# One weight sum of the seven-product blocks, moved from VectorE to GpSimd

## The chip, the cores and the metric

The kernel runs on one core of a Trainium2 chip. The metric is the device time of one execution in microseconds; of several runs the median is given. Profiles are of one execution each.

## What is computed

One decoder layer on 256 tokens of width 2048, in fp32: a SwiGLU feed-forward (width 5632) added at half weight, a token mixer, a second such feed-forward, and a final RMS norm. What matters here is the feed-forward:

```python
def swiglu_ffn(x, w_gate, w_up, w_down):
    return (jax.nn.silu(x @ w_gate) * (x @ w_up)) @ w_down

x = x + FFN_RESIDUAL_SCALE * swiglu_ffn(rms_norm(x, ffn1_norm[l]),
                                        ffn1_w_gate[l], ffn1_w_up[l], ffn1_w_down[l])
...                                     # the mixer
x = x + FFN_RESIDUAL_SCALE * swiglu_ffn(rms_norm(x, ffn2_norm[l]),
                                        ffn2_w_gate[l], ffn2_w_up[l], ffn2_w_down[l])
```

## The kernel before

**Precision.** Every fp32 matrix product is made of three products of a rounded type (fp32r). A weight tile is loaded raw by SyncE's DMA queue (SP), as 128 partitions by 4 x 512 columns (1 MB). ScalarE casts it to a high part `hi` in two halves of 1024 columns, VectorE subtracts it from the raw tile to get the low part `lo` in one instruction of 2048 columns, and TensorE multiplies hi by hi, hi by lo and lo by hi (`parts_of`, `multiply`). In the profile these are `hi_g_p`, `lo_g_p` and so on: g, u, d for the gate, up and down weights; `_p` for the products of the blocks described next, `_x` for their usual products, and no suffix for tiles outside the blocks.

**Seven products for eight.** For pairs of 512-row by 512-column weight tiles in a 2 x 2 arrangement (rows r0, r1; two column groups), `seven` computes the product of a 2 x 2 block of token tiles with a 2 x 2 block of weight tiles in seven products, at the price of sums of weight tiles. The token side's sums are made once (`seven_of`). The weight side has four sums in each block, in this order:

- `w11 = w12 - w11`, in two halves of 1024 columns, for product 4;
- `w11 = w22 - w11`, for product 5;
- `w12 = w22 - w12`, for product 6;
- `w11 = w21 - w11`, for product 3: this is the fourth.

Each writes over a raw tile, which is then cast and split as above. Between them stand the usual products of two further row tiles (`b2`, `b3` with the second column group, `a2`, `a3` with the first). The order of TensorE's work in a block is product 0, 4, b2, 5, b3, 6, 2, a2, 3, a3, 1. TensorE adds up in four PSUM banks a, c, e, d; ScalarE copies some of them out.

**Where blocks stand.** Each feed-forward runs five steps, each with a gate block and an up block over two column groups of 512; after the first, third and fifth step a down block is run over the hidden units so far. That makes 5 x 2 + 3 = 13 blocks in each feed-forward, 26 in all. The mixer between the two feed-forwards uses no such blocks.

**Tiles.** `w11` and `w12` stand in a pool of two buffers of their own (`kept`), the other raw tiles of a block in a pool of three (`raws`). The next block's `w11` takes the buffer of this block's `w12`, and the next block's `w12` that of this block's `w11`, so its load on SP waits until the lo of product 3 is made. `w21` takes one of the three buffers of `raws` and is read by the fourth sum and then, as it is, by product 1. The hi and lo tiles have three buffers.

**Order.** A planner lays the queue of each engine by its own costs and by what it takes to be ready; the engines then work their queues in order and wait for each other through semaphores. A few instructions are pinned behind what was issued ahead of them on their engine (`keep_in_program_order`). In the gate blocks of the third and fifth step of each feed-forward (`order=True`) the two halves of product 4's lo and the sum `w12 - ...` of product 6 are pinned. The fourth sum isn't.

ScalarE, VectorE and TensorE are called through a thin wrapper (class `Engine`), so their instructions all appear at line 43, and groups are told apart by the names of tiles. `nc.gpsimd` is called directly.

Of the kernel before, what the change touches and what calls it, by code (L numbers as in the profile page):

```python
# [14 lines left out]
ALU = mybir.AluOpType  # L15
# [34 lines left out]
def hybrid_block(ctx: ExitStack, tc: tile.TileContext, a: dict, out: bass.AP):  # L50
    nc = tc.nc
    Engine.pinned = False
    dve, act, pe = (Engine(tc, e) for e in (nc.vector, nc.scalar, nc.tensor))
# [29 lines left out]
    def bank(name):  # L83
        return psum.tile([P, 512], F32, tag="ps", name=name)

    def f32(ap):
        return ap.bitcast(F32)
# [71 lines left out]
    def load(src, name, pieces=((0, UK),), loaded=None, kept=False):  # L159
        if kept:  # L160
            raw = extra[1].tile([P, UK, CW], F32, tag="kept", name=f"raw_{name}", bufs=2)
        else:
            raw = raws.tile([P, UK, CW], F32, tag="raw", name=f"raw_{name}")
        for i, e in pieces:
            nc.sync.dma_start(raw[:, i:e, :], src[i * P : e * P].rearrange("(j p) c -> p j c", p=P))
            if loaded:
                loaded(i)
        return raw

    def splits_of(name):  # L170
        pool, bufs = splits, 2
        if extra:
            turn_of["split"] += 1
            if turn_of["split"] % 3 == 0:
                pool, bufs = extra[0], 1
        hi = pool.tile([P, UK, CW], F32R, tag="hi", name=f"hi_{name}", bufs=bufs)
        lo = pool.tile([P, UK, CW], F32R, tag="lo", name=f"lo_{name}", bufs=bufs)
        return hi, lo, [(hi[:, j, :], lo[:, j, :]) for j in range(UK)]

    def parts_of(raw, name, pieces=((0, 2), (2, UK)), split=None):  # L180
        hi, lo, blk = splits_of(name)
        for i, e in pieces:
            if split:
                split(i)
            act.copy(hi[:, i:e, :], raw[:, i:e, :])
            if split:
                dve.tensor_tensor(lo[:, i:e, :], raw[:, i:e, :], f32(hi[:, i:e, :]), op=ALU.subtract)
        if not split:
            dve.tensor_tensor(lo, raw, f32(hi), op=ALU.subtract)
        return blk  # L190
# [4 lines left out]
    def stationary(tile, t):  # L195

        return [(tile[:, j, t * P : (t + 1) * P], tile[:, j, S + t * P : S + (t + 1) * P]) for j in range(UK)]
# [33 lines left out]
    def multiply(targets, blk, apart=False, middle=None):  # L231


        more = dict(skip_group_check=True) if apart else {}
        for ps, st, begin, _ in targets:
            for j in range(UK):
                pe.matmul(ps, st[j][0], blk[j][0], start=begin and j == 0, stop=False, **more)
                pe.matmul(ps, st[j][1], blk[j][0], start=False, stop=False, **more)
        if middle:
            middle()  # L240
        for ps, st, _, end in targets:
            for j in range(UK):
                pe.matmul(ps, st[j][0], blk[j][1], start=False, stop=end and j == UK - 1, **more)
        if len(targets) == NT:
            onward()
# [159 lines left out]
    def seven(w, rows, cols, sf, xs, name, keep, done, between=None, ready=None, whole=True, order=False):  # L405


        a, c, e, d = (bank(f"ps_{name}_{n}") for n in "aced")

        def get(u, n, kept=False):  # L410
            src = w[u * UK * P : (u + 1) * UK * P, cols[n] : cols[n] + CW]
            return load(src, f"{name}_{u}{n}", kept=kept)

        (r0, r1), two = rows, len(xs) > 1
        w11, first = ready or (get(r0, 0, True), None)
        w12 = get(r0, 1, True)
        b2, w22 = get(xs[0][0], 1), get(r1, 1)
        b3 = get(xs[1][0], 1) if two else None
        a2, w21 = get(xs[0][0], 0), get(r1, 0)
        a3 = get(xs[1][0], 0) if two else None  # L420

        def snap(ps, n):
            s = keep(f"{n}_{name}")
            act.copy(s, ps)
            return s

        def product_of(i, raw, ps, begin=False, end=True, blk=None):
            multiply([(ps, sf[i], begin, end)], blk or parts_of(raw, f"{name}_p{i}"), True)

        def usual(i, raw, n, *targets):  # L430

            blk = parts_of(raw, f"{name}_x{i}{n}")
            multiply([(ps, stationary(xs[i][1], t), b, z) for ps, t, b, z in targets], blk, True)

        product_of(0, w11, a, True, blk=first)
        s1 = None if whole else snap(a, "s1")
        if whole:
            act.copy(d, a)
        hi, lo, blk = splits_of(f"{name}_p4")
        for i in (0, 2):  # L440
            o = slice(i, i + 2)
            dve.tensor_tensor(w11[:, o], w12[:, o], w11[:, o], op=ALU.subtract)
            act.copy(hi[:, o], w11[:, o])
        for i in (0, 2):
            o = slice(i, i + 2)
            ins = dve.tensor_tensor(lo[:, o], w11[:, o], f32(hi[:, o]), op=ALU.subtract)
            if order:
                tc.keep_in_program_order(ins)
        product_of(4, w11, c, True, blk=blk)
        s5 = snap(c, "s5")  # L450
        if between:
            between(0)
        usual(0, b2, 1, (e, 1, True, not two), (c, 0, False, False))
        if between:
            between(1)
        dve.tensor_tensor(w11, w22, w11, op=ALU.subtract)
        product_of(5, w11, a)
        u2 = snap(a, "u2")
        if between:
            between(2)  # L460
        if two:
            usual(1, b3, 1, (e, 1, False, True), (c, 0, False, False))
        ins = dve.tensor_tensor(w12, w22, w12, op=ALU.subtract)
        if order:
            tc.keep_in_program_order(ins)
        product_of(6, w12, a)
        u3 = snap(a, "u3")
        done(1, 1, e, [u3, s5])
        product_of(2, w22, c)
        done(0, 1, c, [u2])  # L470
        usual(0, a2, 0, (d, 0, not whole, False), (a, 1, False, False))
        dve.tensor_tensor(w11, w21, w11, op=ALU.subtract)
        product_of(3, w11, a, end=not two)
        if two:
            usual(1, a3, 0, (a, 1, False, True), (d, 0, False, False))
        done(1, 0, a, [])
        product_of(1, w21, d)
        done(0, 0, d, [] if whole else [s1])

    def ffn(tag, norm, after, opening=False):  # L480
        with (
# [252 lines left out]
            def down(last):  # L734
# [64 lines left out]
                if tag == 1 and m == 5:  # L799
                    prepare()  # L800
                seven(
                    wd, (m, n), (2 * CW, CW), sh, [(u, hidden[u]) for u in others], f"d{tag}_{m}", keep, add,
                    within,
# [6 lines left out]
            for s in range(5):  # L810
                cs = (CW + 2 * s * CW, 2 * CW + 2 * s * CW)
                sg = {}

                def total(ps, tiles):
                    for p in tiles[1:]:
                        dve.tensor_tensor(tiles[0], tiles[0], p, op=ALU.add)
                    if not tiles:
                        return ps
                    dve.tensor_tensor(tiles[0], ps, tiles[0], op=ALU.add)
                    return tiles[0]  # L820

                def gate(t, n, ps, tiles):
                    g = total(ps, tiles)
                    sg[t, n] = tiles[0] if tiles else keep(f"z{tag}_{s}")
                    act.activation(sg[t, n], g, AF.Silu)

                def up(t, n, ps, tiles):
                    dve.tensor_tensor(sg[t, n], total(ps, tiles), sg[t, n], op=ALU.mult)
                    turn_hidden(1 + 2 * s + n, t, sg[t, n], s % 2 == 0)

                def meanwhile(i):
                    if s == 0 and not opening and i != 1:
                        (sums, lambda: normalise(3))[i // 2]()

                seven(wg, (0, 1), cs, sf, xs, f"g{tag}_{s}", keep, gate, meanwhile, ready.pop() if ready else None,
                      s > 0 and (tag, s) != (1, 3), s in (2, 4))
                seven(wu, (0, 1), cs, sf, xs, f"u{tag}_{s}", keep, up)
                if s % 2 == 0:
                    down(s == 4)
# [357 lines left out]
```

## Time and profile before

| | |
|---|---|
| median of 2 runs | 1712.8 us (1712.59 to 1713.0) |
| profiled execution, span | 1710.3 us |
| around the span | 2.5 us to the median |
| TensorE (PE) busy | 1693.6 us, 99% |
| VectorE (DVE) busy | 1480.7 us, 87% |
| ScalarE (ACT) busy | 1174.6 us, 69% |
| GpSimd (POOL) busy | 6.9 us |
| granted TensorE clock | 0.999 |
| DMA | 358.96 MB, 210 GB/s |

Times in the views are microseconds from the span's start. A row of the timeline gives start, duration, engine, line, operation, out<-in, shapes and count; in brackets stands the idle time of the engine just ahead of it and what ended it. A row that ends in x2 or x4 merges that many instructions. A row of the groups gives busy time and the mean of one in ns, then the engine's idle time ahead of the group. A row of the waits gives who waited for whom: total, times, longest.

### The profile page before, as it was taken

How to read it: one execution, taken by the hardware profiler on the slowest of the kernel's cores; microseconds unless marked ns; L12 is line 12 of the kernel's file. 1: busy time of each engine (PE TensorE's matmuls, PEld its weight loads, DVE VectorE, ACT ScalarE, POOL GpSimd, SP SyncE). 2: the span in 40 equal slices, each digit the busy share in tenths (PEclk: the TensorE clock that was granted, in tenths of full speed). 3: DMA queues.
4: the chain of work that ended last, by engine and by line, in shares of the span. 5: the costliest groups of instructions: out<-in, count | busy, mean ns of one | idle time of the engine just before them, and what ended most of it. 6: DMA issues, size and time to landing. Idle time of an engine off the chain costs nothing.

```text
span 1710.3 us, 20215 instructions
## 1 busy us (share of the span) xinstructions
PE 1693.6 (99%) x7795; PEld 1411.2 (83%) x7795; DVE 1480.7 (87%) x1297; ACT 1174.6 (69%) x1493; POOL 6.9 (0%) x32
## 2 busy tenths in 40 slices
PE   8999999999999999999999999999999999999997
PEld 6888888888888888888888888888888888888886
DVE  7998988989889879787986669989989888889796
ACT  7867667776567678775655777686567675677764
POOL 1000000000000000000000000000000000000000
PEclk9999999999999999999999999999999999999999
DMA  8666567585567684855555684685666766566753
GB/s 307 204 230 196 197 222 221 191 281 185 181 210 208 224 267 144 247 172 191 177 191 176 221 273 163 209 275 180 216 219 205 215 197 221 197 215 203 243 200 123
DMA packets 237280, 358.96 MB, mean 210 GB/s; under 512 B 68996, under 2 KB 71424, under 8 KB 237056
## 3 DMA queue, kind: packets, MB, share of 16 engines
q1 hardware_dynamic: 236720, 356.55, 64.6%
q8 instruction: 61, 1.00, 0.2%
q10 hardware_dynamic: 144, 1.05, 0.2%
q14 instruction: 35, 0.29, 0.0%
q0 software_dynamic: 320, 0.07, 0.0%
HBM read 339.82 MB, written 2.10 MB: 200 GB/s over the span
## 4 chain that ended last, share of the span: by engine, by line
PE 92%; ACT 3%; DVE 2%; issue 1%; DMA 1%; SPq 0%; DVEq 0%; ACTq 0%
PE ps_d L43 14%; PE ps_in L43 13%; PE ps_g_a L43 8%; PE ps_u_a L43 8%; PE ps_u_c L43 6%; PE ps_d_a L43 5%; PE ps_o L43 5%; PE ps_g_c L43 5%; PE ps_g_d L43 5%; PE ps_d_c L43 3%; PE ps_u_d L43 3%; PE ps_u_e L43 3%; PE ps_u L43 3%; PE ps_d_d L43 3%; PE ps_g_e L43 2%; PE ps_g L43 2%
## 5 line engine op out<-in xcount | busy, mean ns | idle before, releaser
L43 ACT CAST hi_u_p<-raw_u 128x1024 fp32r<-128x1024 f32 x140 | 141.5, 1047 | 54.4 <-DVE raw_u L43 25.7
L43 ACT CAST hi_g_p<-raw_g 128x1024 fp32r<-128x1024 f32 x132 | 134.0, 1047 | 56.4 <-DVE raw_g L43 27.9
L43 DVE TENSOR_TENSOR lo_u_p<-raw_u,hi_u_p 128x2048 fp32r<-128x2048 f32 (+1 forms) x80 | 160.1, 2020 | 14.1 <-ACT hi_u_p L43 13.6
L43 DVE TENSOR_TENSOR lo_g_p<-raw_g,hi_g_p 128x2048 fp32r<-128x2048 f32 (+1 forms) x75 | 151.7, 2033 | 18.5 <-ACT hi_g_p L43 17.7
L43 PE MATMUL ps_d<-hi_d,h 128*128 128x512 f32 x704 | 167.0, 389 | 0.0
L43 PEld LDWEIGHTS ps_d<-hi_d,h 128*128 128x128 f32 x704 | 132.1, 188 | 27.4
L43 PE MATMUL ps_in<-xT_nm,hi_in 128*128 128x512 f32 x640 | 153.1, 391 | 0.0
L43 PEld LDWEIGHTS ps_in<-xT_nm,hi_in 128*128 128x128 f32 x640 | 117.5, 188 | 23.0 <-ACT tha L43 0.4
L43 DVE TENSOR_TENSOR lo_d<-raw_d,hi_d 128x2048 fp32r<-128x2048 f32 x44 | 100.2, 2289 | 34.9 <-ACT hi_d L43 34.8
L43 ACT CAST hi_d_p<-raw_d 128x1024 fp32r<-128x1024 f32 x84 | 86.2, 1048 | 63.7 <-DVE raw_d L43 23.3
L43 ACT CAST hi_in<-raw_in 128x1024 fp32r<-128x1024 f32 x80 | 80.1, 1046 | 59.3 <-PE ps_in L43 45.8
L43 DVE TENSOR_TENSOR lo_in<-raw_in,hi_in 128x2048 fp32r<-128x2048 f32 x40 | 91.4, 2287 | 33.6 <-ACT hi_in L43 33.3
L43 ACT CAST hi_u_x<-raw_u 128x1024 fp32r<-128x1024 f32 x80 | 81.3, 1047 | 38.9 <-PE ps_u_c L43 26.6
L43 DVE TENSOR_TENSOR lo_d_p<-raw_d,hi_d_p 128x2048 fp32r<-128x2048 f32 (+1 forms) x48 | 96.5, 2021 | 7.6 <-ACT hi_d_p L43 7.3
L43 ACT CAST hi_d<-raw_d 128x1024 fp32r<-128x1024 f32 x88 | 88.9, 1045 | 18.5 <-PE ps_d_d L43 7.6
L43 DVE TENSOR_TENSOR raw_u<-raw_u,raw_u 128x2048 f32<-128x2048 f32 (+1 forms) x50 | 92.3, 1863 | 10.3 <-DMA raw_u<-in_ffn_w_up_dram 9.7
L43 DVE TENSOR_TENSOR lo_g_x<-raw_g,hi_g_x 128x2048 fp32r<-128x2048 f32 x40 | 91.5, 2288 | 10.4 <-ACT hi_g_x L43 10.4
L43 ACT CAST hi_g_x<-raw_g 128x1024 fp32r<-128x1024 f32 x80 | 81.2, 1046 | 24.3 <-DMA raw_g<-in_ffn_w_gate_dram 10.8
L43 DVE TENSOR_TENSOR lo_u_x<-raw_u,hi_u_x 128x2048 fp32r<-128x2048 f32 x40 | 91.4, 2286 | 1.2 <-ACT hi_u_x L43 1.2
L43 DVE TENSOR_TENSOR raw_g<-raw_g,raw_g 128x2048 f32<-128x2048 f32 (+1 forms) x46 | 85.1, 1871 | 5.8 <-DMA raw_g<-in_ffn_w_gate_dram 5.6
L43 PE MATMUL ps_d<-lo_d,h 128*128 128x512 f32 x352 | 87.3, 389 | 0.0
L43 PEld LDWEIGHTS ps_in<-xT_nm,lo_in 128*128 128x128 f32 x640 | 82.1, 191 | 3.1
(408 smaller groups left out, 3678.7 us busy)
## 6 DMA issues: line engine op xcount, KB each, us to landing
raw_d<-in_ffn_w_down_dram SPq DMA_DIRECT2D x88, 1024.0 KB, 5.7
raw_u<-in_ffn_w_up_dram SPq DMA_DIRECT2D x87, 1024.0 KB, 5.3
raw_g<-in_ffn_w_gate_dram SPq DMA_DIRECT2D x86, 1024.0 KB, 5.4
raw_in<-in_w_in_dram SPq DMA_DIRECT2D x40, 1024.0 KB, 5.1
raw_o<-in_w_out_dram SPq DMA_DIRECT2D x16, 1024.0 KB, 5.1
xres<-in_x_dram SPq DMA_DIRECT2D x4, 512.0 KB, 7.6
raw_u<-in_ffn_w_up_dram SPq DMA_DIRECT2D x2, 512.0 KB, 9.4
raw_g_first<-in_ffn_w_gate_dram SPq DMA_DIRECT2D x1, 1024.0 KB, 11.9
```

What stands on the lines that cost most here:

```text
L43: ins = getattr(self.engine, name)(*args, **kwargs)
```

## The change

The fourth weight sum of every block is issued to GpSimd's queue in place of VectorE's. Operands, tile and operation are the same.

```diff
         product_of(2, w22, c)
         done(0, 1, c, [u2])
         usual(0, a2, 0, (d, 0, not whole, False), (a, 1, False, False))
-        dve.tensor_tensor(w11, w21, w11, op=ALU.subtract)
+        nc.gpsimd.tensor_tensor(w11, w21, w11, op=ALU.subtract)
         product_of(3, w11, a, end=not two)
         if two:
             usual(1, a3, 0, (a, 1, False, True), (d, 0, False, False))
```

## The prediction

> **What bounds the kernel now.** I read the page from the top: busy times and the chain that ended last; then PE's waits, because an engine that is 99% busy can only lose or gain what it idles.
>
> ```profile
> span 1710.3 us, 20215 instructions
> ...
> PE 1693.6 (99%) x7795; PEld 1411.2 (83%) x7795; DVE 1480.7 (87%) x1297; ACT 1174.6 (69%) x1493; POOL 6.9 (0%) x32
> ...
> PE 92%; ACT 3%; DVE 2%; issue 1%; DMA 1%; SPq 0%; DVEq 0%; ACTq 0%
> ```
>
> TensorE is the bound: 1693.6 of 1710.3 us, and 92% of the chain. It idles 16.7 us in all, most of it at the two ends of the kernel. VectorE is the fullest of the others, but 229.6 us of its span are free, and ScalarE has more. GpSimd (POOL) has next to nothing to do. So the question is not how much work moves, but whether a piece that TensorE needs comes later than it is needed.
>
> ```profile
> PE ps_g_a L43 <- DVE lo_g_p L43: 1.8, 4, 0.6
> ```
>
> This row of PE's waits is the only one in which TensorE waits for VectorE: 1.8 us, in four waits of 0.6 us at most. That is the whole visible prize for unloading VectorE.
>
> **The change part by part. What goes.** One subtract per block leaves VectorE's queue. The two groups below (by shape) hold the whole-tile weight sums of the up and gate products.
>
> ```profile
> L43 DVE TENSOR_TENSOR raw_u<-raw_u,raw_u 128x2048 f32<-128x2048 f32 x30 | 68.7, 2290 | 8.9 <-DMA raw_u<-in_ffn_w_up_dram 8.5
> L43 DVE TENSOR_TENSOR raw_g<-raw_g,raw_g 128x2048 f32<-128x2048 f32 x28 | 63.9, 2288 | 5.8 <-DMA raw_g<-in_ffn_w_gate_dram 5.6
> ```
>
> Up has ten blocks with three whole-tile sums each, which is the x30; gate has ten as well (the first tile of two of them has another name), and down has six: 26 blocks. So VectorE is freed of 26 x 2.29 = 59.5 us and falls to about 1421 us, 83%. It also no longer stands in line for the fourth sum's operand: most of the 8.5 and 5.6 us of idle time above are VectorE at the head of its queue waiting for w21 to land. None of this is on the path, since TensorE does not wait for it; its value is at most the 1.8 us above.
>
> **What comes.** 26 GpSimd instructions of 128x2048 fp32, two inputs. The trace has no such instruction; the nearest rows are these.
>
> ```profile
> L1005 POOL MEMSET zx<- 128x3 f32 x8 | 0.6, 100 | 729.5 <-ACT pair L43 690.8 <-DVE xc L43 38.4 <-ACT xs L43 0.3
> ...
> masks.py:199 POOL TENSOR_SCALAR_AFFINE_SELECT ident<-ident 128x128 f32<-128x128 f32 x1 | 0.3, 313 | 0.1
> masks.py:197 POOL MEMSET ident<- 128x128 f32 x1 | 0.2, 204 | 0.3 <-POOLq L1184 0.3
> ```
>
> A memset costs 100 ns for nothing and (204 - 100) / 125 = 0.83 ns per column written. One read and one write cost (313 - 100) / 128 = 1.66 ns per column, so a read adds 0.83. For 2048 columns: 3.5 us if the second read runs beside the first, 100 + 2048 x 2.49 = 5.2 us if it is a third pass. Neither end is nearer, so I estimate R = 4.4 us, the middle, against VectorE's 2.29. [...]
>
> **Where the latency falls.** GpSimd's queue holds nothing else here (its memsets belong to the mixer), so the instruction starts when w21 lands. Behind it wait, on ScalarE, the two hi casts of product 3 and the casts and PSUM copies queued after them; then VectorE's lo of product 3; then TensorE; and on SP the next block's w12, whose tile that lo frees. A typical gate block, VectorE and then TensorE:
>
> ```profile
> 464.33 2.29 DVE L43 TENSOR_TENSOR raw_g<-raw_g,raw_g 128x2048 f32<-128x2048 f32 x1 [1.60 <-DMA raw_g<-in_ffn_w_gate_dram]
> 466.54 2.28 DVE L43 TENSOR_TENSOR lo_g_p<-raw_g,hi_g_p 128x2048 fp32r<-128x2048 f32 x1
> ...
> 473.14 2.28 DVE L43 TENSOR_TENSOR lo_g_p<-raw_g,hi_g_p 128x2048 fp32r<-128x2048 f32 x1
> ```
>
> ```profile
> 472.71 1.07 PE L43 MATMUL ps_g_c<-lo_g_p,xs 128*128 128x512 f32 x4
> ...
> 480.87 1.07 PE L43 MATMUL ps_g_a<-lo_g_p,x 128*128 128x512 f32 x4
> ```
>
> The fourth sum runs at 464.33, as w21 lands. The lo at 466.54 belongs to product 2, read at 472.71; the one at 473.14 to product 3, done at 475.42 and read at 480.87: 5.45 us early. A sum that ends R - 2.29 = 2.1 us later is covered by that. In one place it is not:
>
> ```profile
> 1085.43 2.29 DVE L43 TENSOR_TENSOR raw_g<-raw_g,raw_g 128x2048 f32<-128x2048 f32 x1
> ...
> 1088.17 3.88 ACT L43 CAST hi_g_p<-raw_g 128x1024 fp32r<-128x1024 f32 x4
> ...
> 1090.19 4.49 DVE L43 TENSOR_TENSOR lo_g_p<-raw_g,hi_g_p 128x2048 fp32r<-128x2048 f32 x2 [0.27 <-ACT hi_g_p L43]
> ...
> 1092.55 1.17 PE L43 MATMUL ps_g_a<-lo_g_p,x 128*128 128x512 f32 x4
> ```
>
> This is the first gate block of the second FFN. The sum ends at 1087.72, two casts run from 1088.17 to 1090.1, the first lo ends at about 1092.45, TensorE reads it at 1092.55: nothing to spare but the 0.45 us ahead of the casts and the 0.2 us by which GpSimd may start sooner. Cost: about R - 2.8 = 1.6 us.
>
> **What the two engines do to each other.** No row shows GpSimd reading a large tile while VectorE works, so this is an unknown with two ends. One end: they do not disturb each other, and the bill is the 1.6 us. The other end: they take turns, and VectorE stands still for R. Then the next VectorE instruction, which starts 2.2 us after the fourth sum's start today, is late by R - 2.2 = 2.2 us, and what counts is how early it is needed. In the block above product 2's lo ends 3.9 us before its use (468.82 to 472.71): nothing lost. Eight blocks have this order; the first and the last of them, VectorE's row and TensorE's:
>
> ```profile
> 114.18 2.29 DVE L43 TENSOR_TENSOR lo_u_p<-raw_u,hi_u_p 128x2048 fp32r<-128x2048 f32 x1
> ```
>
> ```profile
> 120.57 1.07 PE L43 MATMUL ps_u_c<-lo_u_p,xs 128*128 128x512 f32 x4
> ```
>
> ```profile
> 1510.72 2.28 DVE L43 TENSOR_TENSOR lo_u_p<-raw_u,hi_u_p 128x2048 fp32r<-128x2048 f32 x1
> ```
>
> ```profile
> 1517.28 1.07 PE L43 MATMUL ps_u_c<-lo_u_p,xs 128*128 128x512 f32 x4
> ```
>
> They are 4.1 and 4.3 us early. The tight ones are the gate blocks whose order is pinned, four of them, the first and the last shown:
>
> ```profile
> 298.56 2.29 DVE L43 TENSOR_TENSOR raw_g<-raw_g,raw_g 128x2048 f32<-128x2048 f32 x1 [0.53 <-DMA raw_g<-in_ffn_w_gate_dram]
> 300.77 4.49 DVE L43 TENSOR_TENSOR lo_g_p<-raw_g,hi_g_p 128x2048 fp32r<-128x2048 f32 x2
> ```
>
> ```profile
> 303.57 1.07 PE L43 MATMUL ps_g_a<-lo_g_p,xs 128*128 128x512 f32 x4
> ```
>
> ```profile
> 1552.89 4.49 DVE L43 TENSOR_TENSOR lo_g_p<-raw_g,hi_g_p 128x2048 fp32r<-128x2048 f32 x2
> ```
>
> ```profile
> 1556.30 1.07 PE L43 MATMUL ps_g_a<-lo_g_p,xs 128*128 128x512 f32 x4
> ```
>
> Here product 6's lo comes next, is done at 303.05 and 1555.15 (half of each pair), and is read 0.5 and 1.1 us later; with about 0.9 as the mean, each of the four costs R - 3.1 = 1.3 us, 5.2 together. Turns therefore cost 1.6 + 5.2 = 6.8 us at R = 4.4, 2.3 at 3.5 and 10.8 at 5.2. Below nothing, the 1.8 us are the limit. Between the ends 1.6 and 6.8 no row decides; I take 4, the middle.
>
> [...]
>
> **The sum**: 1710.3 + 4 = 1714.3 for the span. The medians' 1712.8 lies 2.5 us above the profiled span (what is around it), so 1717 on the clock that counts.
>
> **The rivals.**
> *Hidden altogether*: no turns, the tight place absorbed or the 1.8 us won. For it: the 229.6 us of free VectorE time and 5.45 us of lead. Against it: the 0.1 us of lead at 1092.55. 1711 to 1714.
> *The queues come out in another order*: the planner lays each queue by its own costs, and a piece that sits on another engine shifts what is ready when. For it: TensorE idles so little that the present order is a good one, and pieces with leads of 0.1 and 0.5 us exist. Against it: the data dependences are the same. If in 8 of 26 blocks a tight lo comes behind one more 2.29 us instruction, 8 x 2.2 = 18 us: 1731; I give it 1722 to 1746.
> *A slow GpSimd with turns, slower by over 2%*: with the two engines taking turns, every block begins to pay beyond a certain R: the eight blocks like 464.33 from R = 2.2 + 3.9 = 6.1 us, and four up blocks, the first and the last below, from 2.2 + 3.6 = 5.8 (the next piece ends at 347.97 and 1601.02, read at 351.62 and 1604.57):
>
> ```profile
> 345.69 2.28 DVE L43 TENSOR_TENSOR lo_u_x<-raw_u,hi_u_x 128x2048 fp32r<-128x2048 f32 x1
> ```
>
> ```profile
> 351.62 1.07 PE L43 MATMUL ps_u_d<-lo_u_x,x 128*128 128x512 f32 x4
> ```
>
> ```profile
> 1598.74 2.28 DVE L43 TENSOR_TENSOR lo_u_x<-raw_u,hi_u_x 128x2048 fp32r<-128x2048 f32 x1
> ```
>
> ```profile
> 1604.57 1.07 PE L43 MATMUL ps_u_d<-lo_u_x,x 128*128 128x512 f32 x4
> ```
>
> At R = 7.2: 4 x 4.1 + 4.4 + 8 x 1.1 + 4 x 1.4 = 35 us, 2% of 1712.8 and about what a measurement of this kernel can tell from no change. At R = 9 it is 4 x 5.9 + 6.2 + 8 x 2.9 + 4 x 3.2 = 66 us, 1779. For it: R is not measured. Against it: my rows reach to 5.2.
>
> **How the numbers follow.** Forecast 0.47 (1714 to 1722), hidden 0.22, other order 0.20, slow GpSimd 0.10, faster by over 2% 0.01: that would need 1678.5 us, below the 1693.6 that TensorE is busy. Slower by over 2% is 0.10, within 2% the remaining 0.89. The range 1710 to 1740 (its low end is the hidden case's 1711 less the 0.4 us between the runs, rounded down) leaves out the slow GpSimd, the top of the other order (0.05) and the 0.01.
>
> **What would show it.** Right: 26 POOL subtracts of 3.5 to 5.2 us at line 472; VectorE near 1421 us busy, or longer by stretched instructions if there are turns; PE still near 1693.6 busy; its waits for VectorE up from 1.8 to about 6, in the pinned gate blocks and near 1092. Turns would show as lo instructions beside a POOL subtract that take 4 us or more instead of 2.29, or start only at its end. Wrong: POOL subtracts of 7 us; TensorE waiting for hi casts in ordinary blocks; a new order of TensorE's products.

## The result, and the profile after

The median of two runs is 1757.94 us (1756.49 to 1759.39) against 1712.8, a ratio of 1.0263 with a 95% interval of 1.0234 to 1.0293. The kernel is 2.6% slower, and the time lies 18 us above the range that was given.

The page of the changed kernel, span and busy times:

```profile
span 1757.6 us, 20241 instructions
...
PE 1708.4 (97%) x7795; PEld 1412.7 (80%) x7795; DVE 1491.4 (85%) x1271; ACT 1172.5 (67%) x1493; POOL 153.2 (9%) x58
```

The number to stop at is VectorE's. It has 26 instructions fewer (1297 to 1271), worth 59.5 us, and is busy for 10.7 us **more**. So some 70 us of its busy time are instructions that stand still: they wait after they have started, and the profile counts that as busy (the lo at 265.94 below stands with 6.49 us in place of 2.29). GpSimd's groups by shape:

```profile
L472 POOL TENSOR_TENSOR raw_u<-raw_u,raw_u 128x2048 f32<-128x2048 f32 x10 | 56.4, 5639 | 370.6 <-DMA raw_u<-in_ffn_w_up_dram 370.6
L472 POOL TENSOR_TENSOR raw_g<-raw_g,raw_g 128x2048 f32<-128x2048 f32 x9 | 52.2, 5804 | 575.9 <-DVE raw_g L43 321.7 <-DMA raw_g<-in_ffn_w_gate_dram 254.3
L472 POOL TENSOR_TENSOR raw_d<-raw_d,raw_d 128x2048 f32<-128x2048 f32 x6 | 30.9, 5155 | 385.9 <-DMA raw_d<-in_ffn_w_down_dram 385.9
L472 POOL TENSOR_TENSOR raw_g_first<-raw_g,raw_g_first 128x2048 f32<-128x2048 f32 x1 | 6.7, 6671 | 66.6 <-DVE lo_g_p L43 66.6
```

The means, 5.2 to 6.7 us, mix two kinds. Ten subtracts that nothing was in the way of take 4.65 to 4.68 us. Those that met a running VectorE instruction take longer: nine take 6.1 to 6.8 us and one 11.0; the six of the down blocks lie between, at 4.7 to 6.0. TensorE's and ScalarE's waits, in the view of what each engine waited for (total, times, longest):

```profile
PE ps_g_a L43 <- DVE lo_g_p L43: 7.7, 8, 1.4
PE ps_u_a L43 <- ACT u_u L43: 5.8, 4, 1.4
PE ps_d_c L43 <- ACT s_d L43: 5.5, 4, 2.5
PE ps_d_c L43 <- DVE hs L43: 4.6, 2, 3.1
PE ps_g_c L43 <- ACT s_g L43: 3.0, 5, 0.8
...
PE ps_g_a L43 <- ACT u_g L43: 2.6, 1, 2.6
PE ps_u_a L43 <- DVE lo_u_p L43: 2.1, 4, 0.8
PE ps_g_c L43 <- ACT hi_g_p L43: 1.9, 4, 0.7
```

```profile
ACT hi_u_p L43 <- POOL raw_u L472: 33.1, 6, 6.9
```

Before, 1.8 us of waits for lo_g_p was all that TensorE waited for VectorE. Now there are the eight kinds of wait for VectorE and ScalarE shown above, each of 1.9 us or more, and more than half of their time is for ScalarE, an engine that the change does not touch. New waits come to about 32 us and TensorE's busy time has grown by 14.8 (1708.4 less 1693.6): together the 47.3 us by which the span grew.

Pairing the k-th matmul of both traces shows that TensorE's order is all but the same, and where the delay builds up. I followed three places. The first is a down block, all engines in order of time:

```profile
180.01 4.78 POOL L472 TENSOR_TENSOR raw_d<-raw_d,raw_d 128x2048 f32<-128x2048 f32 x1 [58.63 <-DMA raw_d<-in_ffn_w_down_dram]
180.22 0.69 DVE L43 SCALAR_TENSOR_TENSOR xres<-ps_d_e,xres 128x512 f32<-128x512 f32 x1
...
180.82 4.52 DVE L43 TENSOR_TENSOR hs<-u_g,hs 128x512 fp32r<-128x512 f32 x1
...
185.39 1.65 PE L43 MATMUL ps_d_c<-hi_d_p,hs 128*128 128x512 f32 x3 [3.08 <-DVE hs L43]
...
186.84 3.62 PE L43 MATMUL ps_d_a<-hi_d_p,hs 128*128 128x512 f32 x8
```

Read the two VectorE rows. The one at 180.22 has one operand in PSUM (ps_d_e) and takes its usual 0.69 us beside the GpSimd subtract. The one at 180.82 has both inputs in SBUF and now lasts until 0.55 us after the subtract ends. In the trace before it was this row:

```profile
177.26 0.68 DVE L43 TENSOR_TENSOR hs<-u_g,hs 128x512 fp32r<-128x512 f32 x1
```

TensorE waits 3.08 us for it. Then eight matmuls that take 1.98 us elsewhere take 3.62; why is in the last section.

The second place is an up block of the third step:

```profile
356.06 2.29 DVE L43 TENSOR_TENSOR lo_u_x<-raw_u,hi_u_x 128x2048 fp32r<-128x2048 f32 x1 [0.38 <-ACT hi_u_x L43]
356.73 6.16 POOL L472 TENSOR_TENSOR raw_u<-raw_u,raw_u 128x2048 f32<-128x2048 f32 x1 [42.44 <-DMA raw_u<-in_ffn_w_up_dram]
...
362.92 1.04 ACT L43 CAST hi_u_p<-raw_u 128x1024 fp32r<-128x1024 f32 x1 [6.89 <-POOL raw_u L472]
363.87 0.58 ACT L43 COPY u_u<-ps_u_a 128x512 f32<-128x512 f32 x1
...
364.50 2.11 PE L43 MATMUL ps_u_a<-hi_u_x,x 128*128 128x512 f32 x8 [1.44 <-ACT u_u L43]
```

Here VectorE came first, and it is GpSimd that stands, until 358.35, and needs 6.16 us. ScalarE's cast for product 3 waits 6.89 us for it, behind the cast stands the PSUM copy u_u, and TensorE waits 1.44 us for that copy before it writes the bank again. No VectorE instruction is late on this path: VectorE's part is the 1.5 us by which it held GpSimd, about as much as that wait of TensorE.

The third is the up block of the second step:

```profile
265.61 4.67 POOL L472 TENSOR_TENSOR raw_u<-raw_u,raw_u 128x2048 f32<-128x2048 f32 x1 [32.81 <-DMA raw_u<-in_ffn_w_up_dram]
265.94 6.49 DVE L43 TENSOR_TENSOR lo_u_p<-raw_u,hi_u_p 128x2048 fp32r<-128x2048 f32 x1 [1.46 <-ACT hi_u_p L43]
...
272.46 0.37 SPq L165 DMA_DIRECT2D raw_u<-in_ffn_w_up_dram  x1
...
277.92 2.00 ACT L43 CAST hi_u_x<-raw_u 128x1024 fp32r<-128x1024 f32 x2 [3.81 <-DMA raw_u<-in_ffn_w_up_dram]
...
295.55 1.19 PE L43 MATMUL ps_g_c<-hi_g_p,xs 128*128 128x512 f32 x4 [0.43 <-ACT hi_g_p L43]
...
300.23 2.11 PE L43 MATMUL ps_g_c<-hi_g_x,x 128*128 128x512 f32 x8 [0.75 <-ACT s_g L43]
```

A lo of 2.29 us lasts 6.49. The tile that it frees is loaded from 272.46; the cast of that load waits 3.81 us, where before it waited this long:

```profile
266.14 2.00 ACT L43 CAST hi_u_x<-raw_u 128x1024 fp32r<-128x1024 f32 x2 [1.29 <-DMA raw_u<-in_ffn_w_up_dram]
```

That cast starts 11.8 us later than before, where the ScalarE rows just ahead of it start 9.3 later. ScalarE stays about 2.1 us behind its old distance up to the next gate block, and there TensorE waits, 30 us after the sum.

### The profile page after: what moved, and what is told of

Same layout as the page of the kernel before. It is cut to its first block, busy times and chain, and to the rows that moved or that the text cites. A ratio compares the mean times of both kernels' runs of the same rounds, so it can differ in the third digit from the quotient of the medians.

```text
span 1757.6 us, 20241 instructions
## 1 busy us (share of the span) xinstructions
PE 1708.4 (97%) x7795; PEld 1412.7 (80%) x7795; DVE 1491.4 (85%) x1271; ACT 1172.5 (67%) x1493; POOL 153.2 (9%) x58
## 5 line engine op out<-in xcount | busy, mean ns | idle before, releaser
L43 DVE TENSOR_TENSOR lo_u_p<-raw_u,hi_u_p 128x2048 fp32r<-128x2048 f32 (+1 forms) x80 | 177.0, 2230 | 16.7 <-ACT hi_u_p L43 16.7
L43 DVE TENSOR_TENSOR lo_g_p<-raw_g,hi_g_p 128x2048 fp32r<-128x2048 f32 (+1 forms) x75 | 162.2, 2171 | 30.3 <-ACT hi_g_p L43 29.7
L43 DVE TENSOR_TENSOR lo_g_x<-raw_g,hi_g_x 128x2048 fp32r<-128x2048 f32 x40 | 108.0, 2701 | 14.3 <-ACT hi_g_x L43 14.1
L43 DVE TENSOR_TENSOR lo_u_x<-raw_u,hi_u_x 128x2048 fp32r<-128x2048 f32 x40 | 96.6, 2416 | 8.2 <-ACT hi_u_x L43 8.2
L472 POOL TENSOR_TENSOR raw_g<-raw_g,raw_g 128x2048 f32<-128x2048 f32 x9 | 52.2, 5804 | 575.9 <-DVE raw_g L43 321.7
L472 POOL TENSOR_TENSOR raw_u<-raw_u,raw_u 128x2048 f32<-128x2048 f32 x10 | 56.4, 5639 | 370.6 <-DMA raw_u<-in_ffn_w_up_dram 370.6
```

The source lines that it names most:

```text
L43: ins = getattr(self.engine, name)(*args, **kwargs)
L472: nc.gpsimd.tensor_tensor(w11, w21, w11, op=ALU.subtract)
```

## The experiments

The theory after this reading: **holding**. While GpSimd reads a tile, a VectorE instruction with two SBUF inputs stands still, and the reverse; VectorE's lateness then spreads through buffers, loads and ScalarE. Its rival: **latency**. Product 3's operand comes some 4 us later, and the queues behind it pay.

To compare the kernels I use how long VectorE was held, which is its busy time less that of the first kernel below, with the difference in instructions allowed for. Instructions that follow each other at once overlap a little in the profile (two lo of 2.29 us stand together as 4.49); without the 26 sums VectorE is busy for 53.4 us less and not 59.5, so a sum counts as 2.05 us here. By this measure the changed kernel's hold is 64.1 us.

**The sum left out.** The line is deleted, and product 3 uses w11 as it stands.

> The fourth sum is left out on every engine (product 3 takes w11 as it stands). This is the floor of the change: all its relief and none of its costs. Both theories: TensorE stays the bound, 1709 to 1714 us. If it comes out near 1758, the loss is that of a changed queue order and not of GpSimd's work.

1711.82 us against 1713.22, ratio 0.999 (0.998 to 0.9999); VectorE busy 1427.3 us. Not having the sum at all is worth 1.4 us. The prediction's prize of at most 1.8 us is confirmed, and another place for the sum can hardly win more.

**Latency without reading.** GpSimd writes the tile and reads two columns of it. The subtraction of the other columns is left out.

```diff
-        nc.gpsimd.tensor_tensor(w11, w21, w11, op=ALU.subtract)
+        nc.gpsimd.tensor_tensor(w11[:, 0, :2], w21[:, 0, :2], w11[:, 0, :2], op=ALU.subtract)
+        for some in (w11, w11, w11[:, 2:]):
+            nc.gpsimd.memset(some, 0.0)
```

> Product 3's tile is made late by GpSimd, but without reading: a two-column subtract that waits for w21 and w11, then memsets of 2048, 2048 and 1024 columns (by their 0.83 ns per column about 4.6 us, as long as the real subtract when undisturbed). The sum itself is left out. Turns theory (VectorE stands still while GpSimd reads): VectorE's instructions stay at 2.29 us, and what is left is the latency, some 2 us in the first gate block of the second FFN and up to 1 us in a few others: 1712 to 1722 us. Latency theory (the casts of product 3 are late and hold up ScalarE's queue, reading or not): most of the 45 us stay, 1740 to 1758.

1715.38 us, ratio 1.0013 (1.0004 to 1.0022). Of its groups on GpSimd, the two largest forms of the up blocks, and the page's line of busy times:

```profile
L474 POOL MEMSET raw_u<- 128x2048 f32 x20 | 36.3, 1813 | 1.2
...
L474 POOL MEMSET raw_u<- 128x1024 f32 x10 | 9.6, 956 | 0.6
```

```profile
PE 1694.3 (99%) x7795; PEld 1411.3 (82%) x7795; DVE 1427.8 (83%) x1271; ACT 1176.1 (69%) x1493; POOL 151.7 (9%) x136
```

Two memsets of 1.81 us, one of 0.96 and the small subtract, 0.20 us where nothing is in its way, make 5.0 us of latency in most blocks, more than the 4.67 of the undisturbed subtract, and VectorE's 1427.8 us are those of the kernel without the sum. Latency costs 3.6 us over that kernel, of 45. The rival falls as the main cause. (The 6 us and more that some real subtracts took are not copied here; they are themselves an effect of holding.)

**Reading, with nobody waiting for the result.** GpSimd's result goes to the dead tile w12, and product 3 takes w11 without the subtraction.

```diff
-        nc.gpsimd.tensor_tensor(w11, w21, w11, op=ALU.subtract)
+        nc.gpsimd.tensor_tensor(w12, w21, w11, op=ALU.subtract)
```

> GpSimd runs the real subtract in the same place, but writes it over w12, which is dead after product 6, and nothing of this block waits for it; product 3 takes w11 as it stands, and no engine makes the sum that is used. So: reading without latency. Turns theory: VectorE's instructions beside it stretch to 4 to 6.5 us, loads and casts come late behind them, 1735 to 1752 us (less than 1758, because ScalarE's head-of-line wait is gone and in the four pinned gate blocks the subtract starts only after product 6's lo). Latency theory: 1710 to 1716.

1784.94 us, ratio 1.0407 (1.0379 to 1.0434). Inconclusive, since the edit did more than was meant: w12's buffer takes the next block's w11, so loads now wait for GpSimd, as SP's waits show.

```profile
SPq L165 <- POOL raw_g L472: 105.4, 10, 13.5
SPq L165 <- POOL raw_u L472: 87.7, 10, 11.5
```

The same question put in another way: the changed kernel, with product 3 taking w21 in place of w11. GpSimd's work and its tile are those of the changed kernel, and the fourth sum is not used.

```diff
-        product_of(3, w11, a, end=not two)
+        product_of(3, w21, a, end=not two)
```

> The changed kernel, but product 3 is made from w21 as it stands, so the result of GpSimd's subtract (same operands, same place, written over w11 as before) is used by nobody: reading without latency, and now without holding up a tile that the next load wants, since w11 is free no later than in the changed kernel. Turns theory: VectorE stands still beside GpSimd as before; what goes is only ScalarE's wait for GpSimd, so 1730 to 1755 us. Latency theory: 1710 to 1716.

1776.86 us against 1713.67, ratio 1.0372 (1.0353 to 1.0392): above the range of both theories. **With nobody computing from the result, the change costs 63 us, not 45.** Its busy times, its largest wait of TensorE and SP's largest wait for GpSimd:

```profile
PE 1717.1 (96%) x7795; PEld 1417.0 (80%) x7795; DVE 1514.9 (85%) x1271; ACT 1171.9 (66%) x1493; POOL 164.7 (9%) x58
```

```profile
PE ps_g_c L43 <- ACT s_g L43: 12.6, 5, 2.9
```

```profile
SPq L165 <- POOL raw_g L472: 88.6, 9, 16.4
```

The last row shows that the flaw of the kernel before it is not gone. w11's buffer is now freed by the subtract itself and no longer by a lo, the next block's load into it waits for GpSimd at the head of SP's queue, and other loads wait behind it: beside the subtract that starts at 480.68 a gate load goes out at 487.96, where the changed kernel sent it at 482.21. So how the 63 us divide between holding and late loads is not shown. What the run does show is more holding: VectorE was held for 87.6 us (1514.9 less 1427.3) against 64.1 in the changed kernel. In the changed kernel 21 of the 26 subtracts stretched a VectorE instruction by over 1 us, here all 26. My reading is that in the changed kernel ScalarE waits for GpSimd, VectorE then runs out of work, and an idle VectorE cannot be held: the wait spares part of the harm. That is argued from the counts, not shown by itself.

**The PSUM copy ahead of the late cast**, against the second place above. First one, then both of product 3's casts were ordered behind the copy u3 (`snap` keeps its instructions in `copied`):

```diff
+        hi, lo, blk = splits_of(f"{name}_p3")
+        for i in (0, 2):
+            ins = act.copy(hi[:, i : i + 2], w11[:, i : i + 2])
+            tc.add_manual_dep(     # in the first of the two kernels only for i == 0
+                ins.ins, copied[-1].ins.name,
+                mybir.DependencyInfo(mybir.DependencyClass.NoSync, mybir.DependencyReason.DATA),
+                reason="copy first",
+            )
+        dve.tensor_tensor(lo, w11, f32(hi), op=ALU.subtract)
-        product_of(3, w11, a, end=not two)
+        product_of(3, w11, a, end=not two, blk=blk)
```

> The changed kernel, with product 3's first cast pinned behind the PSUM copy u3 on ScalarE, so that the copy doesn't wait in line behind a cast that waits for GpSimd. Both theories have TensorE's waits for the copies u_u (5.8 us in four waits) and u_g (2.6 us) go. With the slower start after each wait that is 4 x 1.6 + 2.8 = 9 us: 1747 to 1751. If head-of-line waiting on ScalarE were the main cause, 1735 or less.

1757.9 us, ratio 1.0254 (1.0238 to 1.0269). Nothing moved: the planner put the other cast ahead of the copy, and the wait for u_u is still 5.9 us. The edit did not do what it was for.

> The changed kernel with both casts of product 3 pinned behind the PSUM copy u3 on ScalarE (the try before pinned one of the two, and the planner put the other first, so the order stayed). The waits for u_u and u_g go: 9 us with the slower start after each, 1747 to 1751. Turns theory: no more than that.

1764.0 us, ratio 1.0297 (1.0282 to 1.0312): a miss. The copy goes first now and TensorE's wait for u_u is gone, but the time is not lower. The same block and TensorE's waits:

```profile
356.01 4.68 POOL L474 TENSOR_TENSOR raw_u<-raw_u,raw_u 128x2048 f32<-128x2048 f32 x1 [40.14 <-DMA raw_u<-in_ffn_w_up_dram]
...
356.49 6.35 DVE L43 TENSOR_TENSOR lo_u_x<-raw_u,hi_u_x 128x2048 fp32r<-128x2048 f32 x1 [1.59 <-ACT hi_u_x L43]
```

```profile
PE ps_g_c L43 <- ACT s_g L43: 9.7, 4, 2.5
```

GpSimd now starts ahead of VectorE's lo, which is held to 6.35 us, and what the copy gave comes back as a wait at the start of the next gate blocks (3.0 us in the changed kernel, 9.7 here). VectorE was held for 91.5 us in all. Removing one wait moved the loss, and holding remained.

**Smaller reads.** The subtract in four instructions of 512 columns, and then half of it on each engine:

```diff
-        nc.gpsimd.tensor_tensor(w11, w21, w11, op=ALU.subtract)
+        for j in range(UK):
+            nc.gpsimd.tensor_tensor(w11[:, j], w21[:, j], w11[:, j], op=ALU.subtract)
```

```diff
-        nc.gpsimd.tensor_tensor(w11, w21, w11, op=ALU.subtract)
+        nc.gpsimd.tensor_tensor(w11[:, 2:], w21[:, 2:], w11[:, 2:], op=ALU.subtract)
+        dve.tensor_tensor(w11[:, :2], w21[:, :2], w11[:, :2], op=ALU.subtract)
```

> The changed kernel with GpSimd's subtract cut into four of 512 columns. If GpSimd holds the reading side for a whole instruction, VectorE now stands for about 1.2 us at a time and gets in between: its instructions end after 3.5 us at most instead of 6.5, and the loss shrinks to 1720 to 1740. But each piece can now wait for one of VectorE's 2.29 us, so that product 3 may come up to 7 us later than now: if that decides, 1755 to 1775. If the two share the reading side in small portions anyway, nothing changes: 1755 to 1760.

1736.28 us, ratio 1.0128 (1.0111 to 1.0145). One of the groups:

```profile
L473 POOL TENSOR_TENSOR raw_u<-raw_u,raw_u 128x512 f32<-128x512 f32 x40 | 82.5, 2092 | 334.6 <-DMA raw_u<-in_ffn_w_up_dram 334.6
```

A piece takes 1.29 us alone, so four take 5.2 and more with the turns, yet the loss falls by half, as the holding theory expected, and VectorE is held for 40.9 us. The tiles that are read, and the engines, are the same; what is shorter is one hold. The longest stretches a VectorE instruction by 1.1 us, against 4.5 in the changed kernel.

> GpSimd makes columns 1024 to 2047 of the fourth sum, VectorE the rest. GpSimd's part takes about 2.4 us alone. Turns theory: a stand of 2.4 us is mostly inside the leads that TensorE has (0.9 us in the four pinned blocks, 3.6 and more elsewhere) and inside the slack of the loads: 1714 to 1725 us. If the loss went with the number of GpSimd instructions rather than their length, 1745 to 1758.

1730.35 us, ratio 1.0099 (1.008 to 1.0118), some 5 us over the expectation: half the columns cost 17 us of 45. VectorE was held for some 44 us (1503.2 less 1427.3 and less its own 26 halves of 1.21).

**One kind of block at a time**, to see whether the losses are made block by block: GpSimd for the gate, the up or the down blocks, VectorE for the rest.

```diff
-        nc.gpsimd.tensor_tensor(w11, w21, w11, op=ALU.subtract)
+        sums_here = nc.gpsimd if name.startswith("g") else dve
+        sums_here.tensor_tensor(w11, w21, w11, op=ALU.subtract)
```

> GpSimd takes the sum in the ten gate blocks alone; in the ten up blocks and the six down blocks VectorE makes it as before. Theory: what the change costs is made block by block, where GpSimd's reading holds up VectorE's next instruction, and each block's loss stands in the matmul starts of the changed kernel up to the next GpSimd sum: 13.3 us behind the gate sums (1.6 behind the first, 11.7 behind the nine others), 22.9 behind the up sums, 10.5 behind the down sums. So about 13 us over before here (1725 to 1729), VectorE busy about 1480 us. Rival: lateness is carried from block to block, so a third of the sums alone costs much less than its share: under 7 us (below 1720), and the three kernels of this set together under 30 us.

> GpSimd takes the sum in the ten up blocks alone. Theory of losses made block by block: 22.9 us over before (1733 to 1739), the most of the three. A plain share of VectorE's standing still would give the up blocks no more than the gate blocks (10 of 26 of 46 us, 17.7). Rival of lateness carried from block to block: under 11 us (below 1724).

> GpSimd takes the sum in the six down blocks alone. Theory of losses made block by block: 10.5 us over before (1722 to 1727), with the 3 us stall of TensorE behind the small VectorE product of the hidden values still there (about 185 us and 1208 us into the span) and the granted clock halved for some 4 us behind it. Rival of lateness carried from block to block: under 5 us (below 1718), the stall gone, since VectorE then has its lead.

Against 1713.05: gate 1729.56, ratio 1.0098 (1.0083 to 1.0113); up 1729.48, 1.0092 (1.0058 to 1.0127); down 1721.66, 1.0055 (1.004 to 1.007). Over before that is 16.5, 16.4 and 8.6 us, 41.5 together of the 45. The losses add up, and the rival, which had less than 30 for the three together, is out. My split was off: up was to cost 22.9 and gate 13.3. What an up sum delays is partly paid in the next gate block, but per block all three kinds cost about the same (1.65, 1.64 and 1.43 us). The up kernel's runs spread from 1721.92 to 1735.07, and why is not known; its 16.4 us are uncertain by some 6. The stall of the down block stays when the down sums are alone on GpSimd:

```profile
180.80 1.26 PE L43 MATMUL ps_d_c<-hi_d_p,hs 128*128 128x512 f32 x3 [1.85 <-DVE hs L43]
...
181.85 3.32 PE L43 MATMUL ps_d_a<-hi_d_p,hs 128*128 128x512 f32 x8
```

**One tile read.** GpSimd copies w21 over w11; the subtraction is left out.

```diff
-        nc.gpsimd.tensor_tensor(w11, w21, w11, op=ALU.subtract)
+        nc.gpsimd.tensor_copy(w11, w21)
```

> In all 26 blocks GpSimd copies w21 over w11 in place of the subtraction, so the sum is left out and GpSimd reads one tile from SBUF and writes one; product 3 waits for it as in the changed kernel. What is open: whether it is GpSimd's reading as such that holds VectorE, or only a subtract that reads two tiles. If any reading holds VectorE for as long as GpSimd's instruction lasts, VectorE's busy time grows by about 64 us times the copy's duration over the subtract's 4.66 us: for a copy between the 1.81 us of the memset and 4.66 us, 25 to 64 us over the 1427 us of the kernel without the sum, and the time is 1725 to 1755. If one tile read does not hold VectorE, its busy time stays at 1427 to 1432 us and the time at 1713 to 1718, as with the write alone (1715.4).

1713.42 us against 1713.05, ratio 1.0003 (0.9994 to 1.0013); VectorE busy 1445.6 us. In the timeline:

```profile
176.24 2.16 POOL L472 COPY raw_d<-raw_d 128x2048 f32<-128x2048 f32 x1 [62.02 <-DMA raw_d<-in_ffn_w_down_dram]
...
177.14 1.80 DVE L43 TENSOR_TENSOR hs<-u_g,hs 128x512 fp32r<-128x512 f32 x1
...
256.60 1.90 POOL L472 COPY raw_u<-raw_u 128x2048 f32<-128x2048 f32 x1 [35.63 <-DMA raw_u<-in_ffn_w_up_dram]
...
256.98 3.66 DVE L43 TENSOR_TENSOR lo_u_p<-raw_u,hi_u_p 128x2048 fp32r<-128x2048 f32 x1 [1.46 <-ACT hi_u_p L43]
```

Neither half of what was expected holds in full. A copy of one tile holds VectorE as well: the same hs takes 1.80 us instead of 0.68, the lo 3.66 instead of 2.29. But it costs no time that can be measured. VectorE was held for 18.3 us here and for some 21 us in the kernel with the up sums alone (1481.0 less 1427.3 and less 16 sums of 2.05); one loses 0.4 us, the other 16.4. So the sum of the holds does not decide. What fits is **how long VectorE stands at one place**: 1.7 us at most here, and 2.8 to 4.3 in six of the ten blocks there (the longest lo takes 4.02 us in the one and 6.59 in the other). In the other four up blocks it is GpSimd that was held (6.0 to 6.3 us for the subtract), and TensorE's waits for u_u behind them come to 5.9 us. A copy also delays product 3 by less than a subtract does, so the two kernels differ in more than the hold. With the four pieces, which delay product 3 by more and cost half, the reading is that short holds end within the leads that the kernel has.

## Why the prediction was wrong, point by point

- **The bound and the prize**: right. TensorE bounds the kernel (99% busy before, 97% after), and the sum is worth 1.4 us on VectorE (at most 1.8 was said).
- **What the instruction costs**: 4.4 us estimated, 4.67 measured alone, within 3.5 to 5.2. But its place in time was wrong: it was to start when w21 lands and run through. Where VectorE was first it took 6.1 to 6.8 us, because GpSimd is held too.
- **Latency**: the size was about right, the path was not. R - 2.8 (2.9 by its own terms) gives 2.2 us for 5.0 us of latency, and the kernel that only writes lost 2.2 against the kernel before (1715.38 less 1713.22). The wait was to be for product 3's lo at 1092.55. In the first gate block of the second feed-forward both that kernel and the changed one wait for ScalarE's copy u_g instead, 1.9 and 2.6 us, which stands behind the late cast; and GpSimd was late there because three VectorE instructions went ahead of it (last section). That the number came out is luck.
- **Taking turns** is the step that failed, and in two ways. It was taken as a chance and given the middle of its two ends, 4 us. The trace shows turns in full: hs held to the end of the subtract (4.52 us in place of 0.68), subtracts of 6.2 us behind a running lo. In the second and third place whichever of the two started first took the time it takes alone (the lo 2.29 us, the subtract 4.67) and the other was held (the subtract 6.16 us, the lo 6.49). Where VectorE had a PSUM operand it was not held: xres took 0.69 us beside the subtract. Nor was it beside memsets, which read nothing: VectorE was busy for 1427.8 us, against 1427.3 without the sum. And the upper end of the sum, 6.8 us, was itself too low, by a factor of more than six. The sentence that failed is "what counts is how early it is needed", asked only of the next VectorE instruction and only of TensorE. There the sum was good: the four pinned gate blocks lost 1.3 to 1.6 us each by the paired matmuls, 5.8 together, where 5.2 were worked out. What it left out: small VectorE products that have no lead (hs, 4.6 us in two waits), ScalarE's copies behind a cast that waits (5.8 us for u_u and 2.6 for u_g; the prediction named this queue and gave it no price), loads that start late because a held lo frees its tile late, and the late starts of the next blocks. And it had the eight ordinary blocks at no loss, where by the block kinds each block costs about 1.6 us on the average.
- **The rivals**: the order is all but the same, so "another order" is out; "hidden" is out. "A slow GpSimd with turns" had the turns right, but let ordinary blocks pay only from R = 5.8 us on; the loss came at 4.67 already, because its price, too, asked only for the lead of the next VectorE instruction.
- **What would show it**: VectorE's busy time with stretched lo instructions was named as the sign of turns, and is what the trace shows.

Not settled: how the 14.8 us of added TensorE busy time divide between slower matmuls and the way that their ends are modelled (the stretches of half clock in the last section account for about 5 at most), and why ordering the copy first made it 6 us slower than the changed kernel rather than the same.

## What to carry to other kernels

Moving work to an idle engine is not free by itself: here the two engines held each other (a lo of 2.29 us took 6.49, a subtract of 4.67 us took 6.16). Ask what the new instruction reads, and what the busy engine reads at that time: hs, with two SBUF inputs, was held to 4.52 us, and xres, with a PSUM operand, took its 0.69. Price a hold by its length at one place against the shortest lead of everything that hangs on the held engine (buffers, loads and other engines' queues too), not by the mean load; GpSimd copies of 1.9 us were free here, and subtracts of 4.7 us cost 1.7 us a block on the average. Pieces and halves of the subtract cost less, but none of them beat leaving the sum on VectorE. If an engine's busy time does not fall after work has left it (59.5 us left VectorE here, and its busy time rose by 10.7), suspect that its instructions stand still.

## What the runs showed of the hardware

**Some short stalls of TensorE cost twice.** Stretches of the changed kernel (length, busy times of PE, PEld, DVE, ACT and POOL, the granted clock, then the DMA share and rate):

```profile
185.00:189.00 4.00, 3.61 (x9) 2.83 (x10) 4.00 (x3) 0.00 (x0) 0.00 (x0) 0.50 0.03 9
189.00:192.00 3.00, 3.00 (x10) 2.38 (x9) 0.74 (x1) 1.28 (x2) 0.00 (x0) 0.65 0.94 338
192.00:196.00 4.00, 4.00 (x19) 3.29 (x18) 3.57 (x4) 3.20 (x4) 0.00 (x0) 1.00 0.70 262
...
1115.00:1119.00 4.00, 4.00 (x19) 3.24 (x19) 4.00 (x5) 4.00 (x6) 0.00 (x0) 1.00 0.00 2
...
1208.00:1212.00 4.00, 4.00 (x13) 3.11 (x12) 4.00 (x4) 2.72 (x5) 0.00 (x0) 0.57 0.71 259
```

After the 3.08 us stall that ended at 185.39 the granted clock is 0.50 for 4 us and 0.65 over the next 3, then full again: about 3 us of full clock lost on top of the stall (4 x 0.5 + 3 x 0.35). A stall of 2.47 us that ended at 1207.55 was followed by 0.57 over 4 us. But not every stall does this: behind one of 2.62 us that ended at 1114.49 the clock is 1.00, so the length alone does not decide. In the kernel with the down sums alone a stall of 1.85 us that ended at 180.80 was followed by this too, with a clock of 0.66 over 4 us, as its eight matmuls of 3.32 us and this stretch show:

```profile
180.00:184.00 4.00, 3.20 (x9) 2.48 (x10) 4.00 (x3) 0.33 (x1) 0.20 (x1) 0.66 0.00 0
```

**A waiting engine was not always the next in line.** At the start of the second feed-forward, in the kernel with the copy:

```profile
1076.58 4.48 DVE L43 TENSOR_TENSOR lo_g_p<-raw_g,hi_g_p 128x2048 fp32r<-128x2048 f32 x2
...
1076.71 8.32 POOL L472 COPY raw_g<-raw_g 128x2048 f32<-128x2048 f32 x1 [244.32 <-DVE raw_g L43]
1080.98 2.28 DVE L43 TENSOR_TENSOR lo_g_x<-raw_g,hi_g_x 128x2048 fp32r<-128x2048 f32 x1
```

Three VectorE instructions run back to back from 1076.58 to 1083.26, and the copy, 1.9 us by itself, ends at 1085.03: here GpSimd was let in only when VectorE paused. In the changed kernel the subtract at the same place took 11.0 us, behind three VectorE instructions too. It is not a rule: in the kernel whose sum is not used, a subtract that started at 312.33 was let in between two lo that began 2.2 us apart, and the second lo took 6.8 us. What decides is not known.
